# Where the transpositions stand in a feed-forward's chunk, and two more of the identity

## The chip, the cores and the metric

The kernel runs on one core of a Trainium2 chip (trn2). The metric is the device time of one execution in microseconds; the time before is 1068.07 us, the median of three runs from 1064.77 to 1068.74.

## What is computed

A decoder trunk of two layers on 256 tokens of width 1024, all in float32. Layer 0 mixes the tokens by forgetting attention, layer 1 by latent attention on a compressed key and value. Each layer has two half-step feed-forwards (hidden width 2816), a mixer between them and a gated input embedding behind them, each followed by a layer norm:

```python
def swiglu(x, w_in, w_out):
    h = x @ w_in
    gate, up = h[..., :D_FF], h[..., D_FF:]
    return (jax.nn.silu(gate) * up) @ w_out
...
    for i in range(DEPTH):
        if i == N_A:
            k_nope, k_rope, v_shared = shared_kv(x, kv_w_down, kv_norm, kv_w_up, cos, sin)
        x = post_norm(x, 0.5 * swiglu(x, ffn1_w_in[i], ffn1_w_out[i]), ln_g[i, 0], ln_b[i, 0])
...
        x = post_norm(x, 0.5 * swiglu(x, ffn2_w_in[i], ffn2_w_out[i]), ln_g[i, 2], ln_b[i, 2])
```

## The kernel before

**Products.** Every float32 matrix is split into a high part (ScalarE, L207, L519) and the remainder (VectorE, L208, L523), and a product is three matmuls: high by high, high by low, low by high (`mm3`, L498). They are issued by line 506, `mm`; the trace tells them apart by the tile that they write: `h` and `tr` are rings of two PSUM banks each, `y` a ring of four. A transposition is a TensorE instruction that moves a 128x128 block through the identity (`transpose`, L510).

**The feed-forward** (`ffn`, L615) goes through the hidden width in eleven chunks of 256 columns. A chunk's first product by `HT` (L687) has the weights as the stationary operand: four quarters (u = 0 to 3), each on one weight tile, each of 8 `mm3`, so 24 matmuls of 128x256; 96 in a chunk. The two banks come from ring `tr` or `h` in turn. Then `close` (L704) takes silu of the gate half, multiplies by the other half, and splits the result, which is already transposed for the second product. The second product of a chunk is `W` (L713), with 512-wide moving operands: 24 matmuls into the four `y` banks.

**The order** is by groups of chunks, (2, 3, 4), (5, 6, 7), (8, 9, 10) (`GROUPS`, L45): first products of a group, then the second products that are due (L754 to L767). A feed-forward that follows a layer norm begins chunks 0 and 1 differently (`H`, L623, by `moving`, L542): there the activations are stationary, the weights move in 512 columns, and what comes out is not transposed. Those two chunks need a transposition later: `T` (L675), four transpositions, one copy on ScalarE and one subtraction on VectorE. The very first feed-forward ("cold", at the start of the kernel, when the weights are still arriving) begins with `first` (L628): chunk 0's 96 matmuls of 128x256, on input that comes transposed from memory, and chunk 1 by `HT`.

**The step inside a chunk.** `HT` takes a function `what`. The first chunk of each group gets one (`turns`, L747): `T(0)` at chunk 2, `T(1)` at chunk 5, and at chunk 8 the transpositions of the layer's embedding input (`ple_transpose`, L789) or of the keys and values (`kv_transpose`, L1286). In the cold feed-forward nothing is left to transpose; at chunks 5 and 8 it gets `spare` (L610), four transpositions of the identity into a bank that nobody reads. `HT` calls `what` when u is 1, that is behind the first 24 of its 96 matmuls. `first` calls `spare` once, ahead of everything.

**Who orders the rest.** `Stream` (L119) plans the weight stream by estimated engine times. `use` (L310) hands out a weight tile and may start one split of a later tile (`pump`, L302), and a split that ends a group of tiles starts the next load on SyncE's queue (`split_done`, L253). `transpose` and `parts` (L513) add to the estimates. In `first` the planner is held (`S.hold`), and one split is started by hand behind each quarter but the first.

Of the kernel before, what the change touches and what calls it, by code (L numbers as in the profile page):

```python
# [413 lines left out]
class Trunk:  # L414
# [192 lines left out]
        self.ln_apply(t, st, eps)  # L607


    def spare(self, ring):  # L610
        tr = self.bank(ring)
        for k in range(4):
            self.transpose(tr[:, 128 * k : 128 * k + 128], self.ident)

    def ffn(self, li, which, lni, kv=False, ple=False, at=None, cold=False):  # L615
# [12 lines left out]
        def first():  # L628

            ps = [self.bank("h") for _ in range(2)]  # L630
            key = lambda u: ("win", li, which, 0, u)

            def xs(k):
                def f():
                    self.parts(
                        self.xT[:, :, 0, k, :], self.xT[:, :, 1, k, :],
                        self.xraw[:, k, :].rearrange("p (t c) -> p t c", c=128),
                    )

                return f  # L640

            S.hold = True
            self.spare("tr")
            for u in range(4):
                if u == 0:
                    head = (("hi", 0, 0, 256), xs(0), ("lo", 0, 0, 256), ("both", 0, 256, 512))
                else:
                    head = (xs(2 * u), ("both", 0, 0, 512))
                S.split_pieces(key(u), head + (xs(2 * u + 1), ("both", 1, 0, 512)))
            S.lend("fs")  # L650
            for u in range(4):
                w = self.use(key(u))
                for kk in range(2):
                    k = 2 * u + kk
                    for i, j in ((0, 0), (1, 0), (0, 1)):
                        for b in range(4):
                            self.mm(
                                ps[b // 2][:, 256 * (b % 2) : 256 * (b % 2) + 256],
                                w[:, j, 512 * kk + 128 * b : 512 * kk + 128 * b + 128], self.xT[:, :, i, k, :],
                                (k, i, j, b % 2) == (0, 0, 0, 0), (k, j, b % 2) == (7, 1, 1),  # L660
                            )
                if u:
                    S.split()
            S.hold = False
            close(0, ps)

# [20 lines left out]
        def HT(c, what=None):  # L687
            ring = "tr" if c % 2 == cold else "h"
            ps = [self.bank(ring) for _ in range(2)]
            for u in range(4):  # L690
                if u == 1 and what:
                    what()
                w = self.use(("win", li, which, c, u))
                for kk, b in ((kk, b) for kk in range(2) for b in range(4)):
                    k = 2 * u + kk
                    o = ps[b // 2][:, 256 * (b % 2) : 256 * (b % 2) + 256]
                    col = slice(512 * kk + 128 * b, 512 * kk + 128 * b + 128)
                    self.mm3(
                        o, lambda i: w[:, i, col], lambda i: self.xT[:, :, i, k, :],
                        k == 0 and b % 2 == 0, k == 7 and b % 2 == 1,  # L700
                    )
            close(c, ps)

        def close(c, ps):  # L704
            gt = self.tl([128, 768], F32, "P", 2)[:, 0:512]
            nc.scalar.activation(gt, ps[0], AF.Silu)
            nc.vector.tensor_tensor(gt, gt, ps[1], op=ALU.mult)  # L707
            self.S.busy(act=512, dve=512)
            o = self.tl([128, 2, 512], F32R, "g4", 5)
            self.parts(o[:, 0, :], o[:, 1, :], gt)  # L710
            gT[c] = o
# [18 lines left out]
        if cold:  # L730
            first()
        else:
            H(0, 0, sweeps=SW_H00)
            S.stop = ("win", li, which, 2, 0) if kv else None

            def other():
                self.XT(1)
                S.stop = None

            H(1, 0, HAT, other, SW_H10)  # L740
            if kv:
                self.kv_down(1)
            H(0, 1, sweeps=SW_H01)
            H(1, 1)
        n = NCH
# [8 lines left out]
        for i, group in enumerate((((1,) + GROUPS[0]) if cold else GROUPS[0],) + GROUPS[1:]):  # L754
            for c in group:
                for f in at.get(c, ()):
                    f()
                if c == 4:
                    self.load_gb(li, lni)
                HT(c, turns[i] if c == group[0] else None)  # L760
            if i == 1 and kv:
                self.flush()
                self.kv_transpose_rope()
            if i == 2 and ple:
                self.ple_project(li)
            while late and (late[0] <= group[-1]) and not (i == 0 and late[0] == 1 and not cold):
                W(late.pop(0), both)  # L767
# [959 lines left out]
```

## Time and profile before

| | us |
|---|---|
| median of three runs | 1068.07 |
| the three runs | 1064.77, 1068.07, 1068.74 |
| the profiled execution | 1068.29 |
| its span, first to last instruction | 1066.5 |
| TensorE busy in it | 1055.5 |
| VectorE busy | 716.6 |
| ScalarE busy | 547.1 |

The profile follows one execution. Its page gives each engine's busy time and share of the span, the chain of work that ended last followed back from the end, and groups of instructions by line, engine and tiles with their count, busy time, the mean of one in ns, and the engine's idle time ahead of them. The chain in order of time lists start, length and what ran; a row such as "PE h L506 x96" is one run of 96 matmuls that write `h`. A matmul's own duration is longer than its distance to the next, because matmuls are pipelined; the distance (length of a row by its count) is what counts here. Weight loads (PEld) run beside matmuls. The granted clock is 0.999 of the full one over the span.

### The profile page before, as it was taken

How to read it: one execution, taken by the hardware profiler on the slowest of the kernel's cores; microseconds unless marked ns; L12 is line 12 of the kernel's file. 1: busy time of each engine (PE TensorE's matmuls, PEld its weight loads, DVE VectorE, ACT ScalarE, POOL GpSimd, SP SyncE). 2: the span in 40 equal slices, each digit the busy share in tenths (PEclk: the TensorE clock that was granted, in tenths of full speed). 3: DMA queues.
4: the chain of work that ended last, by engine and by line, in shares of the span. 5: the costliest groups of instructions: out<-in, count | busy, mean ns of one | idle time of the engine just before them, and what ended most of it. 6: DMA issues, size and time to landing. Idle time of an engine off the chain costs nothing.

```text
span 1066.5 us, 17452 instructions
## 1 busy us (share of the span) xinstructions
PE 1055.5 (99%) x7188; PEld 968.3 (91%) x7188; DVE 716.6 (67%) x1031; ACT 547.1 (51%) x831; POOL 66.0 (6%) x94
## 2 busy tenths in 40 slices
PE   9999999999999999999999999999999999999996
PEld 8989999899889999998899898988999889898986
DVE  6675654888797545457976464578887887454566
ACT  5564543666656434453555454435776566354431
POOL 0000000232300000000230000000000000000000
PEclk9999999999999999999999999999999999999999
DMA  8885653454348745454487555422444568565502
GB/s 289 306 301 210 241 186 129 159 163 153 120 153 291 266 168 198 158 183 142 154 294 275 190 197 172 157 72 104 148 154 158 198 244 308 181 206 180 194 1 79
DMA packets 33091, 199.57 MB, mean 187 GB/s; under 512 B 3698, under 2 KB 5490, under 8 KB 12148
## 3 DMA queue, kind: packets, MB, share of 16 engines
q1 hardware_dynamic: 33012, 198.47, 52.8%
q8 instruction: 56, 0.92, 0.3%
q14 instruction: 23, 0.19, 0.1%
HBM read 197.40 MB, written 1.05 MB: 186 GB/s over the span
## 4 chain that ended last, share of the span: by engine, by line
PE 96%; ACT 1%; DVE 1%; issue 1%; POOL 0%; DMA 0%; SPq 0%; DVEq 0%; ACTq 0%; POOLq 0%
PE y L506 36%; PE h L506 35%; PE tr L506 23%; PE tr L510 2%; DMA raw<-in_w_dram 0%; PE h L510 0%; PE tr L1110 0%; ACT hl L207 0%; DVE x L598 0%; POOL fs L980 0%; POOL fs L973 0%; ACT P L1524 0%; DVE qk L523 0%; DVE tr L1514 0%; ACT qk L519 0%
## 5 line engine op out<-in xcount | busy, mean ns | idle before, releaser
L208 DVE TENSOR_TENSOR hl<-raw,hl 128x1024 fp32r<-128x1024 f32 (+3 forms) x260 | 306.3, 1196 | 144.5 <-ACT hl L207 143.9
L207 ACT ACTIVATE hl<-raw 128x1024 fp32r<-128x1024 f32 (+3 forms) x260 | 263.0, 1032 | 180.1 <-PE y L506 98.9
L506 PE MATMUL h<-xT,hl 128*128 128x256 f32 x1584 | 189.7, 279 | 0.8 <-DVE qk L523 0.3
L506 PEld LDWEIGHTS h<-xT,hl 128*128 128x128 f32 x1584 | 185.9, 190 | 2.4 <-ACT hl L245 0.9
L506 PE MATMUL y<-hl,g 128*128 128x512 f32 x792 | 185.6, 390 | 0.0
L506 PEld LDWEIGHTS y<-hl,g 128*128 128x128 f32 x792 | 147.5, 188 | 29.8
L506 PE MATMUL tr<-xT,hl 128*128 128x256 f32 x1464 | 171.5, 277 | 0.0
L506 PEld LDWEIGHTS tr<-xT,hl 128*128 128x128 f32 x1464 | 169.3, 188 | 0.5
L506 PE MATMUL h<-hl,xT 128*128 128x512 f32 (+2 forms) x294 | 65.2, 373 | 0.0
L506 PEld LDWEIGHTS h<-hl,xT 128*128 128x128 f32 x294 | 51.9, 188 | 9.7 <-DVE xT L523 0.3
L506 PE MATMUL y<-hl,xT 128*128 128x512 f32 (+3 forms) x330 | 59.7, 331 | 0.0
L506 PEld LDWEIGHTS y<-hl,xT 128*128 128x128 f32 x330 | 50.1, 188 | 5.6 <-ACT xT L519 0.4
L590 POOL TENSOR_TENSOR rs<-ve,mhalf 128x1 f32<-128x1 f32 x16 | 15.1, 943 | 623.0 <-DVE ve L589 623.0
L523 DVE TENSOR_TENSOR g<-P,g 128x512 fp32r<-128x512 f32 x38 | 26.3, 693 | 26.6 <-ACT g L519 26.6
L506 PE MATMUL y<-hl,otb 128*128 128x512 f32 x168 | 43.5, 398 | 0.0
L519 ACT ACTIVATE xT<-tr 128x512 fp32r<-128x512 f32 x28 | 16.2, 597 | 48.8 <-PE tr L510 48.8
L519 ACT ACTIVATE g<-P 128x512 fp32r<-128x512 f32 x38 | 24.0, 632 | 32.8 <-DVE P L707 32.8
L208 DVE TENSOR_TENSOR otb<-raw,otb 128x1024 fp32r<-128x1024 f32 (+1 forms) x22 | 26.7, 1215 | 20.2 <-ACT otb L207 20.2
L208 DVE TENSOR_TENSOR qk<-raw,qk 128x1024 fp32r<-128x1024 f32 (+2 forms) x23 | 27.9, 1211 | 15.9 <-ACT qk L207 15.9
L506 PEld LDWEIGHTS y<-hl,otb 128*128 128x128 f32 x168 | 30.1, 188 | 5.4
L207 ACT ACTIVATE otb<-raw 128x1024 fp32r<-128x1024 f32 (+1 forms) x22 | 22.9, 1040 | 22.0 <-PE y L506 10.8
L207 ACT ACTIVATE qk<-raw 128x1024 fp32r<-128x1024 f32 (+2 forms) x23 | 24.0, 1045 | 16.1 <-PE tr L506 6.6
(273 smaller groups left out, 1429.7 us busy)
## 6 DMA issues: line engine op xcount, KB each, us to landing
raw<-in_ffn_in_dram SPq DMA_DIRECT2D x85, 1024.0 KB, 5.0
raw<-in_ffn_out_dram SPq DMA_DIRECT2D x44, 1024.0 KB, 4.9
raw<-in_pg_dram SPq DMA_DIRECT2D x8, 1024.0 KB, 4.7
raw<-in_mo_dram SPq DMA_DIRECT2D x8, 1024.0 KB, 4.8
raw<-in_kq_dram SPq DMA_DIRECT2D x8, 640.0 KB, 4.0
gb<-in_ln_g_dram SPq DMA_DIRECT2D x8, 512.0 KB, 5.9
gb<-in_ln_b_dram SPq DMA_DIRECT2D x8, 512.0 KB, 7.9
raw<-in_fk_dram SPq DMA_DIRECT2D x4, 1024.0 KB, 5.0
```

Of the source, the lines that this page charges most:

```text
L207: nc.scalar.activation(hi, src, AF.Copy)
L208: nc.vector.tensor_tensor(lo, src, hi.bitcast(F32), op=ALU.subtract)
L506: self.nc.tensor.matmul(out, lhsT, rhs, start=start, stop=stop)
L510: self.nc.tensor.transpose(out, in_, self.ident)
L519: self.nc.scalar.activation(hi, src, AF.Copy)
L523: self.nc.vector.tensor_tensor(lo, src, hi.bitcast(F32), op=ALU.subtract)
L590: nc.gpsimd.tensor_tensor(rs, ve, self.mhalf, op=ALU.pow)
```

## The change

`HT` calls `what` ahead of its first quarter and no longer between the first and the second. That moves the four transpositions, the copy and the subtraction of eleven places: chunks 5 and 8 of all four feed-forwards and chunk 2 of the three that are not cold. `spare` takes the number of its transpositions, and `first` calls it with two, into ring `tr`, behind the second quarter of chunk 0.

```diff
-    def spare(self, ring):
+    def spare(self, ring, n=4):
         tr = self.bank(ring)
-        for k in range(4):
+        for k in range(n):
             self.transpose(tr[:, 128 * k : 128 * k + 128], self.ident)
...
                 if u:
                     S.split()
+                if u == 1:
+                    self.spare("tr", 2)
             S.hold = False
...
             ps = [self.bank(ring) for _ in range(2)]
+            if what:
+                what()
             for u in range(4):
-                if u == 1 and what:
-                    what()
                 w = self.use(("win", li, which, c, u))
```

## The prediction

> **What bounds the kernel now.** I read the page first: its head, then the chain that ended last, then the groups.
>
> ```profile
> span 1066.5 us, 17452 instructions
> PE 1055.5 (99%) x7188; PEld 968.3 (91%) x7188; DVE 716.6 (67%) x1031; ACT 547.1 (51%) x831; POOL 66.0 (6%) x94
> PE 96%; ACT 1%; DVE 1%; issue 1%; POOL 0%; DMA 0%; SPq 0%; DVEq 0%; ACTq 0%; POOLq 0%
> L506 PE MATMUL h<-xT,hl 128*128 128x256 f32 x1584 | 189.7, 279 | 0.8 <-DVE qk L523 0.3
> L506 PE MATMUL tr<-xT,hl 128*128 128x256 f32 x1464 | 171.5, 277 | 0.0
> ```
>
> TensorE is busy for 99% of the span and carries 96% of the chain. The two groups in which the feed-forward's first product runs stood idle for 0.8 and 0.0 us, so weights, transpositions' results and buffers all come in time. What an edit is worth here is therefore told by how many instructions TensorE has and by how closely one follows the other, and for the second the chain in order of time is the view. Its columns are start in us, length in us, and what ran.
>
> ```profile
> 18.20 11.31 PE tr L506 x96
> ...
> 52.12 11.31 PE h L506 x96
> 63.42 27.22 PE y L506 x120
> 90.64 2.83 PE tr L506 x24
> 93.91 8.17 PE tr L506 x72
> 102.08 10.88 PE h L506 x96
> 112.96 10.88 PE tr L506 x96
> 123.84 16.34 PE y L506 x72
> 140.18 2.83 PE h L506 x24
> 143.44 8.17 PE h L506 x72
> ...
> 548.53 2.74 PE tr L506 x24
> ...
> 625.75 10.89 PE h L506 x96
> 636.85 21.80 PE y L506 x96
> ...
> 978.95 2.83 PE tr L506 x24
> ```
>
> A row with h or tr and 96 is one chunk of 256 hidden columns: 96 products of 128x256, all of one shape. They have **two paces**: 11.31/96 = 117.8 ns in chunks 1 to 4 of the first feed-forward (first and last of four equal rows), 10.88/96 = 113.3 ns later. The change of pace has a place. At 90.64 the first quarter of chunk 5 still takes 2.83/24 = 117.9 ns; then come four transpositions (the gap from 93.47 to 93.91); the rest takes 8.17/72 = 113.5, and chunks 6 and 7 run at 113.3. After the 512-wide products of the second matrix (rows y, 16.34/72 = 226.9 ns) chunk 8 begins slowly again, 2.83 for its quarter, and is quick behind its transpositions. The last feed-forward's chunk 8 begins in the same way at 978.95. So the slow pace comes from a run of 512-wide products at 227 ns (and from the cold start), and four transpositions end it.
>
> That is an association in time, so I looked at what else could make it. The stretches of the trace, with TensorE's busy time, granted clock, share of the DMA engines and GB/s:
>
> ```profile
> 12.60:18.20 5.60, 5.60 (x50) 1.00 1.04 416
> 29.50:40.81 11.31, 11.31 (x99) 1.00 0.63 234
> 112.96:123.84 10.88, 10.88 (x98) 1.00 0.66 230
> ```
>
> The granted clock is 1.00 in all three, and the DMA engines are as busy in a slow chunk (0.63) as in a quick one (0.66). Neither clock nor transfers explain the two paces.
>
> **The change part by part.**
>
> *Two transpositions after the second quarter of chunk 0.* They come when 48 of its 96 products are done; as 48 slow ones take 5.65 us and chunk 1 begins at 18.20, that is about 12.6 us into the span, where the clock is already 1.00; 48 products and chunks 1 to 4 follow, up to the row y at 63.42. Their cost: two transpositions stand in the trace between a chunk and its second products, from 625.75 + 10.89 = 636.64 to 636.85, that is 0.21 us; half of the four's 0.44 us says 0.22. They read the identity only, so nothing has to arrive for them; they write one bank that is overwritten later by TensorE itself. I take +0.21. If they bring the quick pace: 4 x (11.31 - 10.88) = 1.72 us in chunks 1 to 4 and 48 x 4.5 ns = 0.22 us in chunk 0. Net -1.73 us. The bounds are +0.21 (no effect) and -1.73. I take -1.73, the nearer row being the four transpositions of chunks 5 and 8, which always worked, though with four.
>
> *The moved step, chunks 5 and 8 of the four feed-forwards* (eight places). Each place keeps its four transpositions and their 0.44 us; only the 24 products ahead of them change sides. If these run at the quick pace, 2.83 becomes 10.88/4 = 2.72: -0.11 us each, -0.88 in all.
>
> *The same in chunk 2 of the last three feed-forwards.* Here the first quarter is quick already: 2.74/24 = 114.2 ns at 548.53. The gain is 0.02 each, -0.06 in all.
>
> *What the moved step issues.* Four transpositions on TensorE, one copy on ScalarE, one subtraction on VectorE; no DMA. It goes past the call that fetches the first quarter's weights, and with it past what that call may start: one split of a later weight tile on ScalarE and VectorE, and, when that ends a group, a load on SyncE. These now stand behind the copy instead of ahead of it. The times around chunk 5 of the second feed-forward and chunk 2 of the same:
>
> ```profile
> 324.74 0.41 DVE L672 TENSOR_TENSOR P<-P,h 128x256 f32<-128x256 f32 x1
> ...
> 384.27 1.23 DVE L208 TENSOR_TENSOR otb<-raw,otb 128x1024 fp32r<-128x1024 f32 x1 [4.20 <-ACT otb L207]
> 386.39 0.60 ACT L519 ACTIVATE g<-tr 128x512 fp32r<-128x512 f32 x1 [2.15 <-PE tr L510]
> ```
>
> VectorE had idled for 4.20 us before its split and ScalarE for 2.15 before the copy, so an exchange of 0.6 us between them is hidden; uncovered it would cost at most those 0.60 us at a place, 6.6 us at eleven, but the idle column of the groups (0.8 and 0.0) says that the splits run far enough ahead. I cost it at nothing. The only operand that is young is chunk 0's in the step at chunk 2: its last product ended at 324.74 + 0.41 = 325.15, and the step would start at about 328.2, still 3 us later. At chunks 5 and 8 the operands and banks are older by the whole row y. No new wait.
>
> *The sum* against the profiled execution (1068.29 us, of which 1066.5 are the span): -1.73 - 0.88 - 0.06 = **-2.7 us**, so 1065.6. The median of the three runs is 1068.07, so the same step from there gives **1065.4**.
>
> The Trainium skill ("TensorE: Matmul & The Clock Gate", section "Back-to-back issue gap") lets the distance between warm products follow from their width alone, 262 cycles or about 109 ns at 256. This trace disagrees: 117.8 and 113.3 ns for one width at one clock. By that rule no place would gain and the sum would be the two transpositions alone, +0.2 us.
>
> **The rivals.**
>
> *Transpositions straight behind 512-wide products don't bring the quick pace* (the slower side). In every one of the eleven places the transpositions now stand between 256-wide products; the change puts them directly behind 512-wide ones. Elsewhere the trace has that order:
>
> ```profile
> 726.86 4.13 PE y L506 x18
> 730.99 0.44 PE tr L510 x4
> 731.43 3.54 PE h L506 x30
> ...
> 779.74 3.42 PE h L506 x30
> ```
>
> In the attention, 18 wide products, four transpositions and then 30 of 128x256: 3.54/30 = 118.0 ns, slow. The same 30 at 779.74, behind another neighbour, take 114.0. That is one case, and it speaks for the rival. Against it speaks what wide products do behind transpositions and ahead of chunk 2:
>
> ```profile
> 493.26 9.39 PE y L506 x41
> ...
> 855.32 13.76 PE h L506 x60
> 869.08 2.74 PE tr L506 x24
> ```
>
> Behind transpositions wide products run at 9.39/41 = 229.0 ns, not 227; at 13.76/60 = 229.3 they are followed by a quick quarter (114.2 ns). So transpositions behind wide products do move TensorE out of the 227 state, into the one from which short products become quick. Price: a place that fails loses 72 + 192 products of 4.5 ns, 1.19 us, and its hoped 0.11. All eight: +9.5; the three chunks 2, with 288 products, 1.3 us each: +3.9. With the gain in the first feed-forward kept: 1068.07 - 1.7 + 9.5 + 3.9 = 1079.8; with the eight alone 1075.8; with the three alone 1069.4. It decides the sign from three failed places on (-2.7 + 1.3 each), and passes +0.5% at seven.
>
> *Two transpositions are too few.* Behind the two at 636.64 the wide products took 21.80 for 96, 227.1 ns: the 227 state, not the 229 one that four leave. Then the first feed-forward costs +0.21 instead of -1.73: 1068.07 - 0.94 + 0.21 = 1067.3.
>
> *Nothing happens*: the pace follows from something that only coincides with the transpositions, and the change does not do what it is for. 1068.07 + 0.21 = 1068.3. Eight places out of eight against it.
>
> **How the numbers follow.** A measurement of this kernel tells about 0.5% (5.3 us) from no change. The forecast 1065.4 gets 0.45; too few transpositions 0.13; the slower rival at seven places or more 0.26; at one to six places, the three chunks 2 above all, 0.11; nothing 0.03; something that gains over 0.5%, for which I see no term, 0.02. The first, second, fourth and fifth lie within 0.5%: 0.72. Slower 0.26, faster 0.02. The likeliest case's own range is 1062.5 to 1067, the spread of the three runs (1064.77 to 1068.74) laid about it. For 8 in 10 it reaches up to the slower rival at the eight places alone, 1075.8 and a little, and leaves out its worst, near 1080: 1062.5 to 1077.
>
> **What would show it.** In the chain of the changed kernel: the rows of chunks 1 to 4 at 10.88 instead of 11.31 (two transpositions worked) or still 11.31 (too few). At each row y followed by a chunk: a gap of 0.44 and then 96 in about 10.9 (moved step works), or 96 in 11.31 and the next two chunks too (slower rival). At chunk 2 the same. ScalarE's copy of 0.60 should stand some 2.7 us earlier relative to its chunk, and the idle of the two groups should stay under 1 us. The prediction is wrong if a wait appears there, or if the pace after transpositions varies from place to place in a way that no neighbour explains.

## The result, and the profile after

| | before | changed |
|---|---|---|
| median of 14 runs, us | 1066.26 (1064.62 to 1068.74) | 1070.61 (1067.59 to 1073.72) |
| profiled execution, us | 1068.29 | 1070.76 |
| its span, us | 1066.5 | 1068.9 |

The changed kernel takes 1.0041 of the time before, with a 95% interval of 1.0032 to 1.0049: 0.41%, some 4.35 us, slower. The forecast was 2.7 us faster. The page after, its head and the two groups of the first product:

```profile
span 1068.9 us, 17463 instructions
PE 1058.4 (99%) x7190; PEld 971.2 (91%) x7190; DVE 715.8 (67%) x1031; ACT 547.3 (51%) x831; POOL 65.9 (6%) x94
L506 PE MATMUL h<-xT,hl 128*128 128x256 f32 x1584 | 189.1, 279 | 0.3 <-DVE hl L247 0.2
L506 PE MATMUL tr<-xT,hl 128*128 128x256 f32 x1464 | 172.7, 279 | 0.0
```

TensorE has two instructions more and is busy for 2.9 us more; the idle time ahead of the two groups is 0.3 and 0.0 us, so no wait has come in. The loss is in the distance of the products. The chain in order of time (start, length, what ran):

```profile
3.90 6.93 PE h L506 x48
11.05 5.66 PE h L506 x48
16.70 11.31 PE tr L506 x96
...
61.93 27.25 PE y L506 x120
89.62 10.91 PE tr L506 x96
...
326.84 11.31 PE tr L506 x96
...
383.00 10.90 PE h L506 x96
...
548.22 10.90 PE tr L506 x96
...
658.21 11.31 PE tr L506 x96
669.52 11.31 PE h L506 x96
680.83 11.31 PE tr L506 x96
...
869.62 11.31 PE tr L506 x96
...
925.76 11.31 PE h L506 x96
```

The rows show two kinds of places. At 89.62, 383.00 and 548.22 the transpositions stand ahead of the whole chunk and all 96 products run in 10.91 or 10.90, as hoped. At 326.84, 658.21, 869.62 and 925.76 they stand there too, and the chunk takes 11.31, and the next two chunks as well, until the wide products. Seven of the eleven places are quick, four slow.

A slow place costs, with the gap of 0.44 us, 3 x 11.31 = 33.93 against 2.83 + 8.19 + 2 x 10.88 = 32.78 before, so 1.15 us; at chunk 2, where the first quarter took 2.74, 1.24 us. A quick place gains 0.10 (10.91 against 2.83 + 8.18), at chunk 2 0.03. In this execution: 2 x 1.15 + 2 x 1.24 - 6 x 0.10 - 0.03 = +4.15 us. The span grew by 2.4 only, because the row y of the first feed-forward starts at 61.93 instead of 63.42: chunk 0 ended earlier. (Another 0.3 us is saved in the two attentions.) The edit need have no part in the earlier end of chunk 0: in the profiles below whose head is that of the kernel before, the same row starts anywhere from 60.28 to 63.22.

At the head of the kernel there is a second surprise. From 3.90 to 10.83 TensorE ends its first two quarters at the quick pace (the last distances are 113 and 114 ns); behind the two new transpositions it is slow, 5.66/48 = 117.9 ns, and stays so through chunks 1 to 4.

### The profile page after: what moved, and what is told of

Its sections match the earlier page's. It is cut to its first block, busy times and chain, and to the rows that moved or that the text cites. A ratio compares the mean times of both kernels' runs of the same rounds, so it can differ in the third digit from the quotient of the medians.

```text
span 1068.9 us, 17463 instructions
## 1 busy us (share of the span) xinstructions
PE 1058.4 (99%) x7190; PEld 971.2 (91%) x7190; DVE 715.8 (67%) x1031; ACT 547.3 (51%) x831; POOL 65.9 (6%) x94
## 4 chain that ended last, share of the span: by engine, by line
PE 95%; DVE 1%; ACT 1%; issue 1%; POOL 0%; DMA 0%; DVEq 0%; SPq 0%; ACTq 0%; POOLq 0%
PE y L506 35%; PE h L506 34%; PE tr L506 23%; PE tr L510 2%; PE h L510 0%; PE tr L1112 0%; ACT P L1526 0%; DVE hl L208 0%; ACT hl L207 0%; DMA raw<-in_w_dram 0%; DVE x L598 0%; DVE tr L1516 0%; POOL fs L982 0%; POOL fs L975 0%; DVE qk L523 0%
## 5 line engine op out<-in xcount | busy, mean ns | idle before, releaser
L708 ACT ACTIVATE P<-tr 128x512 f32<-128x512 f32 x20 | 12.0, 598 | 41.1 <-PE tr L506 41.1
```

## The theories

**A, chance.** Four transpositions with 256-wide products ahead of them always bring the quick pace. With 512-wide products ahead the pace behind them is drawn anew in each execution. **B, place:** operands, banks or neighbours of the four slow places make them slow. **C:** the pace is drawn everywhere, and the profile of before was a lucky one. **D:** the two transpositions in the first chunk make the loss. **E:** it is the early step itself (its copy and subtraction, the order of the splits). **F:** the pace has nothing to do with the transpositions.

## The experiments

**The changed kernel twice more** (no edit; one profile each), and the kernel before once more.

> The changed kernel once more, for a second profile. Theory A (chance at each place): transpositions directly behind 512-wide products leave the pace of the following 256-wide products to the moment, so the eleven places are drawn anew: again some slow ones (2 to 7 of 11), at other places than the four of the first profile (the chunks at 326.8, 658.2, 869.6 and 925.8 us). Rival B (fixed by the place: its operands, banks and neighbours): the same four are slow and the same seven quick.

> The changed kernel for a third profile. So far 4, 5 and, for the move alone, 3 of 11 places were slow; the chunk at about 658 us in all three, the chunk at about 548 us in none. Pure chance: 2 to 6 slow, and the chunk at 658 slow with a chance of a third. A bias by place: that chunk slow again, and the one at 548 quick again.

> The kernel before once more, for a second profile. Theory A: behind 256-wide products four transpositions always bring the quick pace, so all eleven places have 72 products in 8.16 to 8.20 us and the next two chunks 10.88 each. Rival C (the pace is a lottery everywhere, and the first profile of before was a lucky draw): two or more of the eleven places show 8.48 us and then 11.31. In both, chunks 1 to 4 of the first feed-forward may come out at 11.31 or at 10.88.

The changed kernel took 1070.49 us and 1071.26 us. From the chain of its second profile:

```profile
87.94 11.31 PE tr L506 x96
...
382.57 11.31 PE h L506 x96
...
659.07 11.31 PE tr L506 x96
...
870.62 10.90 PE tr L506 x96
...
925.49 10.90 PE h L506 x96
```

Five slow places, and not the same: 869.62 and 925.76 were slow in the first profile and are quick here (870.62, 925.49); 87.94 and 382.57 have become slow, and the place near 980 us with them. The third profile has four (about 327, 383, 660 and 981 us). B as it was put falls: the same place of the same kernel is slow in one execution and quick in another, the pace is drawn. It isn't drawn evenly, though. Over these three profiles and that of the move alone, the place near 658 us is slow four times of four, the one near 548 never, and three others never. Nor do the places look independent: those near 870 and 925 us agree in all four profiles, and so do those near 383 and 981. Why, stays open.

The kernel before took 1066.24 us; from its chain:

```profile
18.00 10.88 PE tr L506 x96
...
656.78 2.83 PE tr L506 x24
660.04 8.19 PE tr L506 x72
```

All eleven places are quick behind the transpositions, the one near 658 us among them (8.19/72 = 113.8 ns). C falls. But chunks 1 to 4 are quick here (18.00, 10.88), where the profile under the prediction had 11.31: at the head of the kernel the pace is drawn already before the change. There it changes without any transposition, at the pauses in which TensorE waits for its operands: in this profile the products start 118 ns apart up to 8.62, where 0.93 us pass to the next, and 113 ns apart soon behind it; in the profile of the step behind 6 products, below, they start 113 ns apart up to 8.44, where 0.81 us pass, and 118 behind it.

**The move alone, and the two transpositions alone.**

```diff
+            if what:
+                what()
             for u in range(4):
-                if u == 1 and what:
-                    what()
                 w = self.use(("win", li, which, c, u))
```

> Only the moved step, without the two transpositions in the first chunk. Theory A: the whole loss lies here; about a third of the eleven places slow at 1.2 us each and 0.1 us gained at the others: 3 to 6 us slower than before (ratio 1.003 to 1.006). Rival D (the two transpositions in the first chunk make the loss, by taking a quick pace away there): ratio within 0.9995 to 1.001.

```diff
...
                 if u:
                     S.split()
+                if u == 1:
+                    self.spare("tr", 2)
```

> Only the two transpositions behind the second quarter of chunk 0. Theory A: they cost 0.2 us, and after them chunks 1 to 4 are slow or quick by chance; ratio within 0.9985 to 1.001. Rival D (they take a quick pace away that the first chunk mostly has): 1.5 to 2 us slower, ratio 1.0014 to 1.002, and chunks 1 to 4 at 11.31. By the forecast of record they would gain 1.7 us, ratio 0.9984, with chunks 1 to 4 at 10.88.

The move alone: ratio 1.0039 (1.0026 to 1.0052). The two transpositions alone: 0.9989 (0.9981 to 0.9998). The loss is the move's, and D falls. The interval of the two alone holds the 0.9984 of the forecast too, so this time by itself does not speak against that term; the profiles further down do. The chain of the move alone:

```profile
655.41 11.31 PE tr L506 x96
...
728.87 3.42 PE h L506 x30
...
866.94 11.31 PE tr L506 x96
```

Three slow places of eleven, the third near 923 us. And the row at 728.87 is the place in the attention on which the prediction weighed its rival: 30 products behind 18 wide ones and four transpositions. Before the change they took 3.54; here, with the same neighbours, 3.42. That place too is drawn, but far from evenly: in the other thirteen of the fourteen profiles it takes 3.54 or 3.55, so slow is its rule and this row the exception.

**The step behind the first 6, or the first 3, products** instead of 24 (before) or none (changed).

```diff
             for u in range(4):
-                if u == 1 and what:
-                    what()
                 w = self.use(("win", li, which, c, u))
                 for kk, b in ((kk, b) for kk in range(2) for b in range(4)):
+                    if (u, 4 * kk + b) == (0, 2) and what:
+                        what()
```

This is the step behind 6; behind 3 the pair is `(0, 1)`.

> The step comes behind the first 6 of the 96 products (before: 24, changed: 0); nothing in the first chunk. Theory A (a transposition that has 256-wide products on both sides brings the quick pace, one with 512-wide products ahead of it leaves it to chance): all eleven places quick, 18 products gained at 4.5 ns in eight places, 0.65 us: ratio 0.998 to 1.0005. Rival E (what counts is that the step is early: its copy and subtraction, the planner's order, the weights): slow places and a loss as with the move alone, ratio 1.002 to 1.005.

> The step behind the first 3 products, one group of three, instead of 6. If the 512-wide neighbour itself is what leaves the pace to chance: eleven of eleven quick. If the products ahead need some five matmuls to settle, as the distances behind a change of width do (118, 117, 118, 122, 119, then 113): some places slow.

> The step behind the first 3 products, timed. All eleven places were quick in its profile, so 21 products at 4.5 ns are gained in eight places, 0.76 us: ratio 0.9982 to 1.0003; eleven quick places again. A ratio over 1.001 would say that slow places come back in executions that the profile did not show.

Behind 6: 0.9995 (0.9985 to 1.0006). Behind 3: 1065.44 us in the single run, and timed 0.9997 (0.9986 to 1.0008). In all three profiles eleven of eleven places are quick. The place near 658 us, always slow with the step ahead, in a stretch of the chain behind 6 products:

```profile
658.04 0.71 PE tr L506 x6
658.74 0.44 PE h L510 x4
659.18 10.23 PE tr L506 x90
```

and behind 3:

```profile
656.22 0.35 PE tr L506 x3
656.57 0.44 PE h L510 x4
657.01 10.57 PE tr L506 x93
```

90 products in 10.23 and 93 in 10.57 are 113.7 ns each, the few behind the transpositions included. Three narrow products between the wide ones and the transpositions are enough.

Rival E needs a closer look. Both edits leave the step behind the call that fetches the first quarter's weights, so at six of the nine places that have a copy ScalarE splits first and copies then, as in the kernel before. At the three chunks 2 it does not: in the kernel behind 3 products the copy starts at 326.89 and the split at 327.38, in the changed kernel at 326.87 and 327.37 (before: split 328.51, copy 331.42). The chunk, with the order of the changed kernel, is quick:

```profile
326.85 10.57 PE tr L506 x93
```

All twelve chunks 2 are quick in the four profiles with 3 or 6 products ahead (the fourth is the combination below); with none ahead five of twelve are slow. And in the first feed-forward the step has no copy and no subtraction, and ScalarE, VectorE and SyncE run their work in the order of the kernel before; yet the place at 87.94 in the second profile is slow. E falls.

The chunks 2 show something else. The wide products ahead of them are 229 ns apart, and without transpositions in between the first quarter is quick every time (2.74 or 2.75 us for 24, three places of three in both profiles of the kernel before). Four transpositions put in between make five of twelve slow: here the move did not only fail to bring the quick pace, it took it away.

The gain over the kernel before, 0.65 to 0.76 us by the count of products, is within what these comparisons can't tell from none.

**Eight transpositions ahead of the first product**, four of the identity into the chunk's own bank and then the step's own.

```diff
+            if what:
+                for k in range(4):
+                    self.transpose(ps[0][:, 128 * k : 128 * k + 128], self.ident)
+                what()
             for u in range(4):
-                if u == 1 and what:
-                    what()
```

> The step ahead of the first product as in the change, but with four transpositions of the identity ahead of its own four, into the chunk's own bank: eight behind the 512-wide products. Four more cost 0.44 us at eleven places, 4.8 us. Theory A1 (the transpositions need time to settle; eight do it, as six do in the attention): all eleven quick, 4.8 - 0.95 = 3.9 us slower, ratio 1.0036. Theory A2 (the number does not matter, a run of 512-wide products ahead makes it chance): about 4 of 11 slow, 3.9 + 4.8 = 8 to 9 us slower, ratio 1.008.

Ratio 1.0124 (1.0103 to 1.0145). A stretch of the chain:

```profile
664.27 0.43 PE tr L510 x4
664.70 0.44 PE h L510 x4
665.14 2.95 PE tr L506 x25
```

The four more cost 0.43 us, and behind the eight 25 products take 2.95, 118.0 ns. Six of eleven places are slow in this profile. A1 falls: more transpositions don't settle it. Nor does the time since the last wide product explain it: the step's own four stand 0.43 us behind it here, 0.35 us in the kernel behind 3 narrow products. A2 has the kind right and the size too small: 1.008 expected. In the profiled execution (span 1075.9, against 1064.5 in the second profile of before, which was taken on another chip) 11 x 0.43 and six slow places make 4.7 + 7.0 less 0.4 gained, 11.3 of the 11.4 us; the timed runs, 13.9 above, would need some eight slow places, which no profile shows.

**Without transpositions of the identity** in chunks 5 and 8 of the first feed-forward.

```diff
-            lambda: self.spare("h") if cold else T(1, "tr"),
-            self.kv_transpose if kv else self.ple_transpose if ple else lambda: self.spare("tr" if cold else "h"),
+            None if cold else lambda: T(1, "tr"),
+            self.kv_transpose if kv else self.ple_transpose if ple else None,
```

> The kernel before without the four transpositions of the identity in chunks 5 and 8 of the first feed-forward; they compute nothing. Theory A (they bring the quick pace): chunks 5 to 10 all take 11.31, 0.88 us saved and 264 products of 4.5 ns lost twice, 2.4 us: 1.5 us slower, ratio 1.0014. Rival F (the pace recovers by itself within a chunk, or follows from something else at that place): 10.88 again, 0.9 us faster, ratio 0.9992.

Ratio 1.0012 (1.0002 to 1.0021). The chain:

```profile
87.50 11.31 PE tr L506 x96
98.81 11.31 PE h L506 x96
...
137.74 11.31 PE h L506 x96
```

Eight instructions less and a slower kernel: without transpositions the slow pace stays through all six chunks. F falls, and the ratio fits the price of a slow place, 264 products of 4.5 ns (1.0014 was expected).

**Four transpositions in the first chunk; and the best of both edits.**

```diff
...
                 if u:
                     S.split()
+                if u == 1:
+                    self.spare("tr", 4)
```

> Four transpositions of the identity behind the second quarter of chunk 0 instead of two, the step as before. Theory A: they cost 0.44 us and chunks 1 to 4 are quick in the profile (10.88 each); as the kernel before has these chunks slow in one of its two profiles and quick in the other, the mean gain is about half of 1.9 us less 0.44: ratio 0.9985 to 1.0002. If two are as sure as four, the two alone (0.9989) are 0.2 us better than this; if two leave it to chance, this is equal or better.

The step behind 6 products, with two in the first chunk:

> The step behind the first 6 products and the two transpositions in the first chunk. Theory A: the two edits add up, 0.65 us by the step (measured 0.9995 alone) and the two transpositions' mean gain (measured 0.9989 alone): ratio 0.9975 to 0.9995, all eleven places quick. If the gain of the two transpositions was an accident of that call, 0.9990 to 1.0005.

Four: 0.9999 (0.9989 to 1.0009). The combination: 1.0000 (0.9991 to 1.0009), so the two edits don't add up, and the gain of 0.9989 for the two alone did not come again. Two stretches of the chain show why, the two alone first:

```profile
11.62 0.22 PE tr L510 x2
11.84 5.45 PE h L506 x48
```

and the combination:

```profile
11.38 0.22 PE tr L510 x2
11.60 5.66 PE h L506 x48
```

Behind two transpositions the 48 products take 5.45 (quick) in one and 5.66 (slow) in the other, though both were at 113 and 114 ns just ahead of them. In all five profiles with two transpositions the products ahead of them were quick; behind them three are slow and two quick; of the eight without any, six are quick from chunk 1 on. In the one with four it was quick ahead of them and behind. Two transpositions draw the pace anew even between narrow products (five profiles, no more), and at this place there was mostly nothing to gain.

## Why the prediction was wrong

- **What bounds the kernel**: right. TensorE's distance of products is all that moved; no wait came in. The Trainium skill ("TensorE: Matmul & The Clock Gate", section "Back-to-back issue gap") gives the 262 cycles for an isolated product of that width; for a stream of weight loads and products it says that both set the spacing. It names nothing of what ran before them; by that neither the move nor the kernel without the eight transpositions would be slower, and both are (1.0039, 1.0012).
- **The two paces, and what ends the slow one**: right for four transpositions with narrow products ahead, though at the head of the kernel a pause can change the pace as well. In nine profiles that have this order, all 97 places are quick (eleven each, nine where the first feed-forward had none).
- **The moved step, -0.88 and -0.06 us**: the step that failed. It took over, from places with narrow products ahead, that transpositions bring the quick pace, and applied it where wide products are ahead. The gain of a quick place was right (0.10 measured, 0.11 forecast), the price of a slow one too (1.15 and 1.24, forecast 1.19 and 1.3). But of 44 places in four profiles 16 were slow: 11 of 32 in chunks 5 and 8, and 5 of 12 in chunk 2. Four slow places of eleven make 4 x 1.18 less 7 x 0.08, +4.2 us for the move (1.18 and 0.08 are the means over the slow and the quick places); 1.0039 was measured, +4.2. The prediction's last sign of being wrong, a pace that varies from place to place in a way that no neighbour explains, is what came.
- **The argument against the rival**, that wide products behind transpositions run at 229 ns, a state that leads to the quick pace, is where the rival was wrongly set aside: that state leads to the quick pace when the narrow products follow directly (chunk 2 before the change), not when transpositions stand in between (slow in five of twelve). The single direct case of that order was set aside as one case; more profiles would have shown it slow in thirteen of fourteen.
- **The two transpositions, -1.73 us**: failed as well. Chunks 1 to 4 at 11.31 were one execution's draw, not the kernel's habit: they were quick in six of the eight profiles without transpositions there. And two leave the pace to chance. The rival "too few" came nearest, with 0.22 us as their cost, but it left the pace as it was; in three of five profiles a quick pace turned slow behind the two.
- **No new wait, order of splits at nothing**: right. The idle time ahead of the two groups of the first product is 0.3 and 0.0 us after the change, and the chunks 2 behind 3 or 6 products, with the exchanged order, lose nothing.
- **The rivals**: the slower one was the mechanism, at one to six places, the case that was given 0.11. Its sums had whole groups of places fail (the eight, the three, or all), not some of each, another set in each execution. With four slow places and nothing gained at the head its own prices give -0.94 + 4 x 1.3 + 0.21 = +4.5 us.

## What to carry to other kernels

Where TensorE is never idle, a place in the instruction stream can have a pace, and an edit's worth lies in whether the pace behind it is sure or drawn. Before moving something out of a place that always works, find a place in the trace with the new neighbours, and count how often it comes out each way over several profiles; one profile shows one draw. Here the attention held such a place. A habit seen once at the head of this kernel, where the pauses fell differently in each execution, was the least to build on.

## What the runs showed of the hardware

- Products of one shape at the full granted clock (0.997 to 0.999 over the span) have two lasting paces, 113.3 and 117.8 ns at 128x256. A run of 512-wide products at 227 ns directly ahead always led to the slow one (eight places of eight in both profiles of the kernel before), one at 229 ns to the quick one (three of three in both).
- Behind four transpositions the pace is quick in 97 of 97 places if three or more 256-wide products stand ahead of them, in 28 of 44 if 512-wide ones do. Eight behind wide ones: 5 of 11. Two behind quick narrow ones: quick afterwards in 2 of 5.
- Once drawn, the pace holds through 264 to 432 products, and at the head of the kernel it also changed at pauses of 0.8 to 0.9 us. What in the engine makes the two paces, and why some places are drawn less evenly than others, these runs don't show.
